# Weight sums of the up projection's quarters on GpSimd, and a third pair of tiles by quarters in the two middle passes

## The chip, the cores and the metric

The kernel runs on one core of a Trainium2 chip. The metric is device time in microseconds (us). TensorE is called PE here, VectorE DVE, ScalarE ACT, GpSimd POOL and SyncE SP, as in the profile.

## What is computed

A decoder trunk of two layers on 512 tokens of width 1024, in float32. Each layer runs four token mixers side by side on one projection of the normalised input, merges them with gates, and then an MLP with 4096 hidden columns. The change is in the MLP's first matrix:

```python
def squared_relu_mlp(h, w_up, w_down):
    return jnp.square(jax.nn.relu(h @ w_up)) @ w_down
...
        h = rms_norm(x, ln_mlp[l])
        x = x + squared_relu_mlp(h, w_up[l], w_down[l])
```

## The kernel before

**Precision.** A float32 weight chunk is loaded (`raw` or `cr`) and split in two: `whi` is its rounded part, written by ACT (a CAST), and `wlo` the rest, written by DVE as `raw - whi` (`split_w`, line 258). The activations are split too (`hh`/`hl` going in, `ah`/`al` between the matrices). Each product is three matmuls, hi by hi, lo by hi and hi by lo (`mm3`, line 268). There are three buffers each for `whi` and `wlo`, so a split waits until PE has finished with the chunk three before it.

**The MLP** (`mlp`, line 389) goes over the hidden columns in four passes (`PASSES`). A pass makes four pairs of 128-column tiles, t = 0 to 3 (the up part), and then multiplies them with their rows of `w_down` (the down part). The down part is always by quarters, the Strassen-Winograd way: seven products (forms) of half-size blocks in place of eight, with the names A11, S1, S2, S4, S3, A22, A12 in that order. Its blocks of weights are `chain`, `b22`, `sum2` and `raw`. Its four results per pass, c12, c22, c21, c11, are pairs of tiles `co` (three buffers in turn). In passes 1 and 2 they are added to a DRAM tensor by DMAs on POOL's queue (`keep`, line 556, `sum_dram<-co`), in pass 0 written by SP; pass 3 folds them into the output.

**The up part.** An ordinary pair is two tiles of 24 matmuls of 512 columns (lines 493 to 500). A pair whose number is in `SEVEN[p]` goes by quarters (`up_seven`, line 417). Its weights are four 128x512 blocks B11, B12, B22, B21, which SP loads into halves of four `cr` buffers; the other halves take weight sums:

```python
437  sums = {0: ((S1w, B11, B12),), 1: ((S2w, S1w, B22),), 2: ((S3w, B12, B22), (all4, S2w, B21)), 3: ()}
...
442                            for o_, a_, b_ in sums[i]:
443                                with HP():
444                                    V.tensor_add(o_, a_, b_)
445                            ws[i] = split_w(R[i], 512 if i == 3 else 1024, P)
```

So buffer R[0] holds B11 and S1w, R[1] S2w and B22, R[2] S3w and all4, R[3] B21 and B12. Each of the seven forms is 12 matmuls of 256 columns: A11 and S1 use R[0], S2 and S4 R[1], S3 and A22 R[2], A12 R[3]. Between forms, DVE and ACT move partial results out of PSUM: U = copy of A11's bank A, then at line 463 `V.tensor_sub(U2, C, U)`, in the profile `U<-up,U`, which reads bank C after S2 and before S3 adds into that bank; then the parts of F, relu and square. For every pair ACT and DVE then form the split activations: `ah`, `Fs`, `al` (lines 502 to 508).

**What sets the order.** Each engine works through its own queue in order. The order within a queue is made by a scheduler when the program is built; operations under `HP()` (high priority) are placed as early as it can. `cr` buffers (`CRB` = 6) are handed on by the scheduler too: a load into one waits until the split of what it held has ended.

Of the kernel before, what the change touches and what calls it, by code (L numbers as in the profile page):

```python
# [17 lines left out]
ALU = mybir.AluOpType  # L18
# [16 lines left out]
G1K = ((1, 1, 2, 2, 2), (2, 2, 2, 2))  # L35
KORD = ((0, 1, 2, 3, 4, 5, 6, 7), (4, 5, 6, 7, 0, 1, 2, 3))
PASSES = (8, 8, 8, 8)
SEVEN = ((2, 3), (2, 3), (2, 3), (2,))
CRB = 6
BIG = 1e30  # L40

# [12 lines left out]
def chunk_plan(l):  # L54
# [30 lines left out]
    for p, nt in enumerate(PASSES):  # L85

        half = nt // 2 * P
        for t in range(0, half, P):
            parts = 2 if t // P in SEVEN[p] else 1
            for i in range(parts):  # L90
# [80 lines left out]
def trunk(tc, x_in, wall, consts, lps, sgus, out):  # L171
    nc = tc.nc
    at = dict(mm=None, side=False, first=None)
    V, S, G, T_ = (Paced(tc, e, at) for e in (nc.vector, nc.scalar, nc.gpsimd, nc.tensor))
    HP = lambda off=URGENT: tc.high_priority(offset=off)
    plan = [ch for l in range(NL) for ch in chunk_plan(l)]
    with ExitStack() as es:
# [14 lines left out]
        def mmtile(name, tag="mm", bank=None):  # L192
            if bank is None:
                bank = turn[tag]
                turn[tag] = (bank + 1) % 4
            return psum.tile([P, 512], F32, name=name, tag=f"{tag}{bank}")
# [49 lines left out]
        def next_w(raw=None):  # L246
            kk, n = chunk_shape(plan[pos[0]])
            pos[0] += 1
            L = kk * n
            if raw is None:  # L250
                raw = wpool.tile([P, WCH], F32, name="raw", tag="raw", bufs=WB[0])
            src = wall[off[0]:off[0] + P * L].rearrange("(p l) -> p l", l=L)
            off[0] += P * L
            with HP():
                nc.sync.dma_start(raw[:, :L], src)
            return split_w(raw, L, n, V.tensor_copy if pos[0] == 1 else S.copy)

        def split_w(raw, L, n, copy=S.copy):
            hi = wpool.tile([P, WCH], F32R, name="whi", tag="whi", bufs=WB[1])
            lo = wpool.tile([P, WCH], F32R, name="wlo", tag="wlo", bufs=WB[1])  # L260
            with HP():
                copy(hi[:, :L], raw[:, :L])
                r = V.tensor_sub(lo[:, :L], raw[:, :L], hi[:, :L].bitcast(F32))
            at["first"] = r if pos[0] == 1 else None
            return (hi[:, :L].rearrange("p (k n) -> p k n", n=n),
                    lo[:, :L].rearrange("p (k n) -> p k n", n=n))

        def mm3(o, ah, al, bh, bl, start, stop, more=False):

            T_.matmul(o, ah, bh, start=start, stop=False, skip_group_check=more)  # L270
            T_.matmul(o, ah, bl, start=False, stop=False, skip_group_check=more)
            r = T_.matmul(o, al, bh, start=False, stop=stop, skip_group_check=more)
            if not at["side"]:
                at["mm"] = r
# [11 lines left out]
        def tick():  # L286
            at["side"] = True
            for g in list(side):
                if next(g, side) is side:
                    side.remove(g)  # L290
            at["side"] = False
# [97 lines left out]
        def mlp(l, hh, hl, r2, gain, fp, sh, sl):  # L389
# [9 lines left out]
            sums = sum_dram[l]  # L399
            with tc.tile_pool(name="ap", bufs=1) as ap:  # L400
# [6 lines left out]
                def cr():  # L407
                    return ap.tile([P, 1024], F32, name="cr", tag="cr", bufs=CRB)

                def moving(f, k):  # L410

                    if f >= S3:
                        return sh[k][:, f - S3], sl[k][:, f - S3]
                    k, r = k + 4 * (f in (A22, A12)), (row2, row1)[f in (A11, A12)]
                    return hh[k][:, r], hl[k][:, r]

                def up_seven(F):

                    base, sz = off[0], P * 512
                    off[0] += 4 * sz  # L420
                    pos[0] += 4

                    def ld(dst, i, j):
                        o = base + ((i - 1) * 2 + j - 1) * sz
                        with HP():
                            nc.sync.dma_start(dst, wall[o:o + sz].rearrange("(p l) -> p l", l=512))

                    R = [cr() for _ in range(4)]
                    R[1:] = R[2:] + R[1:2]
                    lo, up = slice(0, 512), slice(512, 1024)  # L430
                    B11, S1w, S2w, B22 = R[0][:, lo], R[0][:, up], R[1][:, lo], R[1][:, up]
                    S3w, all4, B21, B12 = R[2][:, lo], R[2][:, up], R[3][:, lo], R[3][:, up]
                    ld(B11, 1, 1)
                    ld(B12, 1, 2)
                    ld(B22, 2, 2)
                    ld(B21, 2, 1)
                    sums = {0: ((S1w, B11, B12),), 1: ((S2w, S1w, B22),), 2: ((S3w, B12, B22), (all4, S2w, B21)), 3: ()}
                    ws = [None] * 4

                    def form(f, o, i, n, first=True):  # L440
                        if ws[i] is None:
                            for o_, a_, b_ in sums[i]:
                                with HP():
                                    V.tensor_add(o_, a_, b_)
                            ws[i] = split_w(R[i], 512 if i == 3 else 1024, P)
                        w_h, w_l = ws[i]
                        for k in range(4):
                            bh, bl = moving(f, k)
                            mm3(o, w_h[:, 4 * n + k], w_l[:, 4 * n + k], bh, bl, first and k == 0, k == 3, not first)
                        tick()  # L450

                    A, B, C, E = (mmtile("up", "ms")[:, 0:256] for _ in range(4))
                    s1, s2 = (hpool.tile([P, 2, 256], F32, name="U", tag=n) for n in ("acc", "sq"))
                    U, U2, W, R5 = s1[:, 0], s1[:, 1], s2[:, 0], s2[:, 1]
                    form(A11, A, 0, 0)
                    with HP():
                        S.copy(U, A)
                    form(S1, B, 0, 1)
                    with HP():
                        S.copy(R5, B)  # L460
                    form(S2, C, 1, 0)
                    with HP():
                        V.tensor_sub(U2, C, U)
                    form(S4, B, 1, 1, False)
                    with HP():
                        V.tensor_add(F[:, A12], B, U2)
                    form(S3, C, 2, 0, False)
                    with HP():
                        V.tensor_sub(W, C, U)
                        V.tensor_add(F[:, A22], W, R5)  # L470
                        S.activation(F[:, 2:4], F[:, 2:4], AF.Relu)
                    form(A22, E, 2, 1)
                    with HP():
                        V.tensor_sub(F[:, A21], E, W)
                        S.activation(F[:, A21], F[:, A21], AF.Relu)
                    form(A12, A, 3, 0, False)
                    with HP():
                        S.activation(F[:, A11], A, AF.Relu)
                        S.activation(F, F, AF.Square)

                for p, nt in enumerate(PASSES):
                    nk = nt // 2
                    ah, al = [], []
                    for t in range(nk):
# [4 lines left out]
                        if t == 1:  # L489
                            early = at["mm"]  # L490
                        if t in SEVEN[p]:
                            up_seven(F)
                        for i in range(0 if t in SEVEN[p] else 2):
                            w_h, w_l = next_w()
# [1101 lines left out]
```

## Time and profile before

| | us |
|---|---|
| median of 3 runs | 1584.31 (1582.98 to 1584.33) |
| the profiled execution | 1584.03 |
| its span | 1582.3 |
| passes 0 to 2 of the first layer's MLP | 81.7, 80.9, 80.9 |
| POOL busy in the whole span | 144.9 |

Times inside the profile are us from the start of the span. A row of instructions has start, duration, engine, line, operation, out<-in, and in brackets the idle time ahead of it with what ended it. L143 is a helper that issues all instructions of the wrapped engines, so rows are told apart by tile names. A duration of PE is modelled and overlaps the next; the spacing of starts tells its pace. Of DVE and ACT the next instruction starts some 0.08 us before the last has ended.

### The profile page before, as it was taken

What the parts mean: (1) busy time and instruction counts of PE and PEld (TensorE: products, weight loads), DVE (VectorE), ACT (ScalarE), POOL (GpSimd) and SP (SyncE); (2) the same over time, 40 slices, a digit from 0 to 9 for tenths busy, and PEclk for the clock granted to TensorE, in tenths of its full rate; (3) what the DMA queues carried; (4) which work ended last, traced back from release to release, by engine and by line L of the source; (5) the groups of instructions that cost most, each with busy time, mean ns of one, the idle gap of its engine ahead of it and who ended that gap; (6) DMA issues with size and microseconds to landing.
All of it is one profiled execution on the core that took longest, in us unless ns stands there. A gap on an engine that the chain in (4) does not pass through costs nothing.

```text
span 1582.3 us, 21761 instructions
## 1 busy us (share of the span) xinstructions
PE 1573.6 (99%) x8091; PEld 1318.2 (83%) x8091; DVE 1226.1 (77%) x2103; ACT 753.9 (48%) x1160; POOL 144.9 (9%) x189
## 2 busy tenths in 40 slices
PE   9999999999999999999999999999999999999999
PEld 7888887888889898988888888887888888889887
DVE  6899997645588777785978999976555887868678
ACT  5553224423357464746545433254233574747462
POOL 1322000000001011111013120000000010111110
PEclk9999999999999999999999999999999999999999
DMA  7533322332347566769455233233223555676692
GB/s 193 146 91 102 101 97 88 104 116 97 104 153 202 166 172 139 198 135 270 131 131 140 81 113 105 84 101 134 86 97 108 172 160 180 167 166 180 145 281 81
DMA packets 77835, 218.22 MB, mean 138 GB/s; under 512 B 8832, under 2 KB 16192, under 8 KB 77728
## 3 DMA queue, kind: packets, MB, share of 16 engines
q1 hardware_dynamic: 60784, 175.54, 34.2%
q0 software_dynamic: 16080, 40.27, 13.0%
q8 instruction: 64, 1.05, 0.3%
q10 hardware_dynamic: 864, 1.01, 0.2%
q14 instruction: 43, 0.35, 0.1%
HBM read 192.10 MB, written 21.01 MB: 135 GB/s over the span
## 4 chain that ended last, share of the span: by engine, by line
PE 71%; DVE 16%; issue 5%; ACT 5%; DMA 2%; POOL 1%; SPq 0%; DVEq 0%; POOLq 0%; ACTq 0%
PE g L143 18%; PE up L143 15%; PE r L143 8%; PE tk L143 7%; PE q L143 6%; PE fm L143 5%; PE p L143 4%; PE wo L143 4%; DVE wlo L143 4%; DVE sco L143 2%; ACT whi L143 2%; DMA raw<-in_wall_dram 1%; DVE Fs L143 1%; DVE m L143 1%; ACT F L143 1%
## 5 line engine op out<-in xcount | busy, mean ns | idle before, releaser
L143 ACT CAST whi<-raw 128x1024 fp32r<-128x1024 f32 (+3 forms) x208 | 228.5, 1100 | 220.6 <-DMA raw<-in_wall_dram 81.7
L143 DVE TENSOR_TENSOR wlo<-raw,whi 128x1024 fp32r<-128x1024 f32 (+3 forms) x209 | 267.6, 1281 | 77.5 <-ACT whi L143 65.2
L143 PE MATMUL g<-hh,whi 128*128 128x512 f32 x512 | 200.6, 392 | 0.0
L143 PE MATMUL g<-hh,wlo 128*128 128x512 f32 x512 | 199.6, 390 | 0.0
L143 PE MATMUL g<-hl,whi 128*128 128x512 f32 x512 | 199.3, 389 | 0.0
L143 DVE TENSOR_TENSOR wlo<-cr,whi 128x1024 fp32r<-128x1024 f32 (+1 forms) x136 | 157.8, 1165 | 45.7 <-ACT whi L143 45.4
L143 ACT CAST whi<-cr 128x1024 fp32r<-128x1024 f32 (+1 forms) x136 | 136.9, 1008 | 105.4 <-PE up L143 40.4
L143 PE MATMUL up<-hh,whi 128*128 128x512 f32 (+1 forms) x456 | 160.4, 352 | 0.0
L143 PE MATMUL up<-hl,whi 128*128 128x512 f32 (+1 forms) x456 | 159.6, 350 | 0.0
L143 PE MATMUL up<-hh,wlo 128*128 128x512 f32 (+1 forms) x456 | 159.6, 350 | 0.0
L143 ACT ACTIVATE gs<-gs 128x512 f32<-128x512 f32 x64 | 40.6, 634 | 200.7 <-DVE gs L143 200.6
L143 PEld LDWEIGHTS g<-hh,wlo 128*128 128x128 f32 x512 | 96.1, 188 | 20.3
L143 PEld LDWEIGHTS g<-hh,whi 128*128 128x128 f32 x512 | 96.1, 188 | 19.8 <-issue 0.2
L143 PEld LDWEIGHTS g<-hl,whi 128*128 128x128 f32 x512 | 96.2, 188 | 19.3
L143 PE MATMUL tk<-whi,hh 128*128 128x512 f32 (+2 forms) x304 | 108.1, 359 | 0.0
L143 PE MATMUL tk<-wlo,hh 128*128 128x512 f32 (+2 forms) x304 | 107.1, 354 | 0.0
L143 PE MATMUL tk<-whi,hl 128*128 128x512 f32 (+2 forms) x304 | 106.3, 352 | 0.0
L143 DVE TENSOR_TENSOR gs<-g,rb 128x512 f32<-128x512 f32 x64 | 44.1, 688 | 78.8 <-PE g L143 78.7
L143 PE MATMUL q<-whi,ah 128*128 128x512 f32 (+1 forms) x260 | 100.7, 391 | 0.1
L143 PE MATMUL q<-whi,al 128*128 128x512 f32 (+1 forms) x260 | 99.8, 389 | 0.1
L143 PE MATMUL q<-wlo,ah 128*128 128x512 f32 (+1 forms) x260 | 99.6, 387 | 0.0
L143 PEld LDWEIGHTS up<-hh,whi 128*128 128x128 f32 x456 | 86.2, 189 | 12.6 <-ACT F L143 1.0
(308 smaller groups left out, 3556.1 us busy)
## 6 DMA issues: line engine op xcount, KB each, us to landing
raw<-in_wall_dram SPq DMA_DIRECT2D x135, 512.0 KB, 3.7
raw<-in_wall_dram SPq DMA_DIRECT2D x64, 640.0 KB, 3.8
cr<-in_wall_dram POOLq DMA_DIRECT2D x48, 512.0 KB, 8.3
cr<-in_wall_dram SPq DMA_DIRECT2D x32, 512.0 KB, 5.5
cr<-in_wall_dram SPq DMA_DIRECT2D x56, 256.0 KB, 2.9
sum_dram<-co POOLq DMA_DIRECT2D x32, 256.0 KB, 6.0
x<-in_x_dram SPq DMA_DIRECT2D x16, 256.0 KB, 5.1
xm_dram<-x SPq DMA_DIRECT2D x16, 256.0 KB, 2.0
```

Of the source, the lines that this page charges most:

```text
L143: r = f(*a, **k)
```

## The change

The four sums of a pair move from DVE to GpSimd and are issued together, after the loads and ahead of all forms, at high priority. And in passes 1 and 2 of each layer pair t = 1 goes by quarters too, so that a middle pass has one ordinary pair and three by quarters.

```diff
-SEVEN = ((2, 3), (2, 3), (2, 3), (2,))
+SEVEN = ((2, 3), (1, 2, 3), (1, 2, 3), (2,))
...
-                    sums = {0: ((S1w, B11, B12),), 1: ((S2w, S1w, B22),), 2: ((S3w, B12, B22), (all4, S2w, B21)), 3: ()}
+                    with HP():
+                        for o_, a_, b_ in (S1w, B11, B12), (S2w, S1w, B22), (S3w, B12, B22), (all4, S2w, B21):
+                            G.tensor_tensor(o_, a_, b_, ALU.add)
                     ws = [None] * 4
 
                     def form(f, o, i, n, first=True):
                         if ws[i] is None:
-                            for o_, a_, b_ in sums[i]:
-                                with HP():
-                                    V.tensor_add(o_, a_, b_)
                             ws[i] = split_w(R[i], 512 if i == 3 else 1024, P)
```

GpSimd's queue in the first layer, from the chain loads of pass 1 to those of pass 2, before (L538 adds a second block of `w_down` onto a loaded one, L540 loads one, L563 adds results to the sums in DRAM):

```order
L538 DMA cr<-in_wall_dram 128x1024
L540 DMA cr<-in_wall_dram 128x1024
L538 DMA cr<-in_wall_dram 128x1024
L540 DMA cr<-in_wall_dram 128x1024
L538 DMA cr<-in_wall_dram 128x1024 x2
L563 DMA sum_dram<-co 128x512 x8
L538 DMA cr<-in_wall_dram 128x1024
L540 DMA cr<-in_wall_dram 128x1024
```

The same place with the change, where the source's line numbers are one less:

```order
L143 TENSOR_TENSOR cr<-cr 128x512 x12
L537 DMA cr<-in_wall_dram 128x1024
L539 DMA cr<-in_wall_dram 128x1024
L537 DMA cr<-in_wall_dram 128x1024
L539 DMA cr<-in_wall_dram 128x1024
L537 DMA cr<-in_wall_dram 128x1024 x2
L143 TENSOR_TENSOR cr<-cr 128x512 x4
L562 DMA sum_dram<-co 128x512 x4
L143 TENSOR_TENSOR cr<-cr 128x512
L562 DMA sum_dram<-co 128x512 x4
L143 TENSOR_TENSOR cr<-cr 128x512 x7
L537 DMA cr<-in_wall_dram 128x1024
```

All twelve sums of pass 1 now stand ahead of its chain loads, and the four sums of pass 2's first pair stand ahead of the writes of pass 1's c12 and c22.

DVE's queue in pass 0, where the up part goes over from ordinary tiles to its first pair by quarters (`cr<-cr 128x512` are sums, `U<-up,U` is line 463), before:

```order
L143 TENSOR_TENSOR Fs<-F,Fs 128x256
L143 TENSOR_TENSOR cr<-cr 128x512 x2
L143 TENSOR_TENSOR al<-Fs,ah 128x1024
L143 TENSOR_TENSOR wlo<-cr,whi 128x1024
L143 TENSOR_TENSOR cr<-cr 128x512 x2
L143 TENSOR_TENSOR wlo<-cr,whi 128x1024
L143 TENSOR_TENSOR Fs<-F 128x512
L143 TENSOR_TENSOR Fs<-F,Fs 128x256
L143 TENSOR_TENSOR al<-F,ah 128x768
L143 TENSOR_TENSOR Fs<-F,Fs 128x256
L143 TENSOR_TENSOR wlo<-cr,whi 128x512
L143 TENSOR_TENSOR U<-up,U 128x256
```

The same place with the change:

```order
L143 TENSOR_TENSOR Fs<-F,Fs 128x256
L143 TENSOR_TENSOR al<-Fs,ah 128x1024
L143 TENSOR_TENSOR wlo<-cr,whi 128x1024 x2
L143 TENSOR_TENSOR Fs<-F 128x512
L143 TENSOR_TENSOR Fs<-F,Fs 128x256
L143 TENSOR_TENSOR al<-F,ah 128x768
L143 TENSOR_TENSOR Fs<-F,Fs 128x256
L143 TENSOR_TENSOR wlo<-cr,whi 128x512
L143 TENSOR_TENSOR U<-up,U 128x256
```

The sums are gone from DVE's queue and the rest keeps its order. In the second and third pair of a middle pass it is the same: two `wlo`, `Fs`, `Fs`, `al`, `Fs`, then `U`.

DVE's queue at the end of pass 1, from c12 (`co<-q`) over c22 (`co<-Z`) to the splits for the last A22 and A12 forms, before:

```order
L143 SCALAR_TENSOR_TENSOR co<-q_5388,t_61,U 128x512
L143 TENSOR_TENSOR wlo<-cr,whi 128x1024
L143 TENSOR_TENSOR cr<-cr 128x512 x3
L143 SCALAR_TENSOR_TENSOR Z<-r_5389,t_61,Z 128x512
L143 TENSOR_TENSOR wlo<-raw,whi 128x1024
L143 TENSOR_TENSOR co<-Z 128x512
L143 SCALAR_TENSOR_TENSOR Z<-r_5390,t_61,Z 128x512
L143 TENSOR_TENSOR wlo<-cr,whi 128x1024
L143 TENSOR_TENSOR co<-Z 128x512
L143 TENSOR_TENSOR wlo<-raw,whi 128x1024
```

With the change:

```order
L143 SCALAR_TENSOR_TENSOR co<-q_5451,t_61,U 128x512
L143 TENSOR_TENSOR wlo<-cr,whi 128x1024
L143 TENSOR_TENSOR wlo<-raw,whi 128x1024
L143 SCALAR_TENSOR_TENSOR Z<-r_5452,t_61,Z 128x512
L143 SCALAR_TENSOR_TENSOR Z<-r_5453,t_61,Z 128x512
L143 TENSOR_TENSOR co<-Z 128x512 x2
L143 TENSOR_TENSOR wlo<-cr,whi 128x1024
L143 TENSOR_TENSOR wlo<-raw,whi 128x1024 x2
```

The second tile of c22 now stands ahead of the `wlo<-cr` of the last A22 form, where it stood behind it.

## The prediction

> **What bounds the kernel now.** I read the page first, then the busy time of the four up/down passes of the first layer, then the instructions around one pair of tiles. Columns of the second block: stretch, its length, busy time and count of PE, PEld, DVE, ACT, POOL, then clock, DMA share, GB/s.
>
> ```profile
> span 1582.3 us, 21761 instructions
> PE 1573.6 (99%) x8091; PEld 1318.2 (83%) x8091; DVE 1226.1 (77%) x2103; ACT 753.9 (48%) x1160; POOL 144.9 (9%) x189
> ```
> ```profile
> 463.10:544.84 81.74, 81.53 (x449) 70.02 (x448) 70.76 (x95) 48.57 (x67) 4.68 (x6) 1.00 0.58 171
> 544.84:625.77 80.93, 80.71 (x433) 69.51 (x433) 62.21 (x78) 46.76 (x62) 7.93 (x10) 1.00 0.63 169
> 625.77:706.71 80.94, 80.72 (x434) 69.52 (x433) 63.25 (x79) 47.79 (x63) 13.13 (x16) 1.00 0.67 166
> ```
>
> The last two are the middle passes that get a third pair. What one matmul costs PE is read from starts, since the durations overlap (start, duration in us):
>
> ```profile
> 706.54 0.39 PE L143 MATMUL up<-hh,whi 128*128 128x512 f32 x1
> ...
> 728.30 0.28 PE L143 MATMUL up<-hh,whi 128*128 128x256 f32 x1
> 728.42 0.28 PE L143 MATMUL up<-hl,whi 128*128 128x256 f32 x1
> ```
>
> From the first up matmul of a pass to the first 256-wide one are 96 matmuls of 512 columns: 21.76/96 = 0.2267 us each. A 256-wide one follows after 0.12 us. A middle pass has 96 up matmuls of 512, 168 of 256 (two pairs of 84) and 168 down matmuls of 512: 264 x 0.2267 + 168 x 0.12 = 80.0 us of its 80.9. So PE sets the pace and only 0.9 us of a pass is waiting. VectorE (DVE) is not far off, though, and while a pair by quarters runs it has no room. This is the second pair of such a pass, on DVE and then PE:
>
> ```profile
> 573.60 1.22 DVE L143 TENSOR_TENSOR wlo<-cr,whi 128x1024 fp32r<-128x1024 f32 x1
> ...
> 578.27 1.23 DVE L143 TENSOR_TENSOR wlo<-cr,whi 128x1024 fp32r<-128x1024 f32 x1 [0.81 <-ACT whi L143]
> 579.41 0.68 DVE L143 TENSOR_TENSOR Fs<-F 128x512 f32<-128x512 f32 x1
> ...
> 580.48 0.95 DVE L143 TENSOR_TENSOR al<-F,ah 128x768 fp32r<-128x768 f32 x1
> 581.34 0.42 DVE L143 TENSOR_TENSOR Fs<-F,Fs 128x256 f32<-128x256 f32 x1
> 581.68 0.42 DVE L143 TENSOR_TENSOR U<-up,U 128x256 f32<-128x256 f32 x1
> ```
> ```profile
> 582.48 0.28 PE L143 MATMUL up<-sh,whi 128*128 128x256 f32 x1
> ```
>
> From 578.27 on DVE never waits. Its U (line 463) reads the PSUM bank that the form S3 then adds into, and S3 is the matmul at 582.48. U ends at 582.10: **0.38 us of slack**. Whatever delays DVE by more than that between 578 and 582 stops PE.
>
> **The change part by part.**
>
> *The third pair.* An ordinary pair is 48 matmuls of 512 columns, 48 x 0.2267 = 10.88 us; by quarters it is 84 of 256, 84 x 0.12 = 10.08. Saving 0.80 us, in two passes of two layers: **-3.2 us**, as PE sets the pace there. But two pairs by quarters in a row have a seam, since the next pair's first form needs the bank that ScalarE has yet to empty:
>
> ```profile
> 576.99 0.28 PE L143 MATMUL up<-sl,whi 128*128 128x256 f32 x1
> 577.11 0.28 PE L143 MATMUL up<-sh,wlo 128*128 128x256 f32 x1
> 577.36 0.38 PE L143 MATMUL up<-hh,whi 128*128 128x256 f32 x1
> 577.58 0.28 PE L143 MATMUL up<-hl,whi 128*128 128x256 f32 x1
> ```
>
> From 577.11 to 577.58 stand two matmuls in 0.47 us where 0.24 is usual: 0.23 us per seam. Three pairs have two seams instead of one: 4 x 0.23 = **+0.9 us**. The loads carry the same bytes (four of 256 KB for two of 512 KB) and come early; ScalarE, busy 47 of 81 us, gets four more operations per pair and hides them.
>
> *The sums on GpSimd.* Four 128x512 adds per pair leave DVE, where one takes about 0.6 us of its queue (two in the 1.29 us row below). GpSimd has this shape as a multiply, beside DVE operations whose usual time is the last row's:
>
> ```profile
> 136.41 1.30 POOL L143 TENSOR_TENSOR wt<-wt,cst 128x512 f32<-128x512 f32 x1 [3.90 <-issue]
> ```
> ```profile
> 136.48 2.03 DVE L143 SCALAR_TENSOR_TENSOR X<-X,c_gc,bigT 128x128 f32<-128x128 f32 x3
> ```
> ```profile
> 923.07 1.47 POOL L143 TENSOR_TENSOR wt<-wt,cst 128x512 f32<-128x512 f32 x1 [3.73 <-DMA wt<-in_sgus_dram]
> ```
> ```profile
> 922.77 1.92 DVE L143 SCALAR_TENSOR_TENSOR X<-X,c_gc,bigT 128x128 f32<-128x128 f32 x3
> 924.99 0.33 DVE L143 SCALAR_TENSOR_TENSOR X<-X,c_gc,bigT 128x128 f32<-128x128 f32 x1
> ```
>
> Three X operations of 0.33 us should take about 1.0 us; both times they took 1.9 to 2.0 when a GpSimd multiply began among them, and 0.9 to 1.0 us went. So a GpSimd operation on two SBUF tensors holds up a DVE operation on two SBUF tensors: I take **1.0 us lost per add that meets a busy DVE**, against 0.6 when DVE did the add itself. Bounds: 0, where DVE would have waited anyway, and 1.30, the whole add. The Trainium skill ("SBUF — State Buffer", section "SBUF: two separate sides") says why: VectorE and GpSimd share a port pair, locked for a whole instruction against a VectorE operation with two SBUF inputs. By that rule the loss would be the whole 1.30 us, and the term of the middle passes below 12 us instead of 8.4; the two rows show about 1.0, and the measurement stands.
>
> Where do the adds fall? Those of the first pair of a pass fall in the pass before, where the buffers come free; there DVE has some 2 us of slack ahead of PE, and I count nothing. Those of the second pair fall beside the ordinary tiles: nothing. Those of the new third pair can't come early. The second add needs the load into the buffer that the split at 573.60 (ended 574.82) gives free, and a load takes 2.9 us:
>
> ```profile
> cr<-in_wall_dram SPq DMA_DIRECT2D x56, 256.0 KB, 2.9
> ```
>
> So it starts at 577.7 at the earliest, and with the third and fourth 1.30 us each behind it the three reach to 581.6, exactly the stretch in which DVE runs wlo, Fs, Fs, al and Fs, all on two SBUF tensors, in front of U. The split that could go at 578.27 gets through some 1.0 us after 577.7, so loses 0.45; the other two cost 1.0 each: 2.45 us, less 0.38 of slack, is **2.1 us of PE waiting** per middle pass: **+8.4 us** for four (0 to 0.75 + 1.3 + 1.3 - 0.38 = 3.0 each, so 0 to 12). In the third pair no add is left, and DVE is level with PE again. ScalarE's cast of each buffer now waits for GpSimd's add in place of DVE's, with the relu and square of the tiles queued behind it; the third pair's third buffer, the one that needs the fourth add, is split a whole pair, 10 us, after the second pair's (at 578.27), so even an add that ends at 583 is in time.
>
> *The first pass of a layer* (two pairs, as before). Here the last two adds of the second pair sit in the DVE queue right in front of the first U:
>
> ```profile
> 485.47 1.29 DVE L143 TENSOR_TENSOR cr<-cr 128x512 f32<-128x512 f32 x2
> 486.68 1.22 DVE L143 TENSOR_TENSOR wlo<-cr,whi 128x1024 fp32r<-128x1024 f32 x1
> ...
> 490.69 0.42 DVE L143 TENSOR_TENSOR U<-up,U 128x256 f32<-128x256 f32 x1
> ```
> ```profile
> 491.20 0.35 PE L143 MATMUL up<-sh,whi 128*128 128x256 f32 x1
> ```
>
> They go (1.2 us), and as GpSimd adds that wait for the same split they meet DVE's queue (2.0 us): 0.8 later, less 0.1 of slack: 0.7, twice: **+1.4 us** (0 to 2.6).
>
> *GpSimd's queue.* At the end of a middle pass four adds now stand ahead of the writes of c12 to the sums in DRAM. DVE's second c22 tile reuses c12's buffer, and DVE's order has it ahead of the split for the second A22 form:
>
> ```profile
> 609.24 0.86 POOL L563 DMA_DIRECT2D sum_dram<-co  x1 [20.39 <-DVE co L143]
> ```
> ```profile
> 608.86 1.21 DVE L143 TENSOR_TENSOR wlo<-cr,whi 128x1024 fp32r<-128x1024 f32 x1
> ...
> 617.78 0.68 DVE L143 TENSOR_TENSOR co<-Z 128x512 f32<-128x512 f32 x1
> ```
> ```profile
> sum_dram<-co POOLq DMA_DIRECT2D x32, 256.0 KB, 6.0
> ```
> ```profile
> 620.33 2.72 PE r L143 x12
> ```
>
> The third add waits for the split that ends at 610.07, so the fourth ends at about 612.7, and the first write leaves 3.5 us later than 609.24. Landed 6.0 us on, at 618.7, it lets c22 go (0.6) and then the split (1.2): 620.5, against PE's need at 620.33. So nothing if the write lands 0.2 us sooner than the median, and 1.1 if the splits that the adds meet there cost them 0.9 us; I take 0 per middle pass, as 0.2 is the nearer.
>
> **The sum**: -3.2 + 0.9 + 8.4 + 1.4 = +7.5 us. The profiled execution took 1584.03 us (its span of 1582.3 and 1.7 around it); the median of three is 1584.31, 0.3 above. So 1584.03 + 7.5 + 0.3 = **1591.8 us**.
>
> **The rivals.** About 0.2%, 3.2 us, is what a measurement of this kernel can tell from no change.
>
> *A, the adds are hidden and PE's saving counts.* If GpSimd gets its turns where DVE waits for ScalarE (such as the 0.81 us ahead of 578.27), only -3.2 + 0.9 = -2.3 us remains: 1582.0. For it: DVE is idle 18 us of a middle pass. Against: none of these gaps lies between 578.27 and U. It decides for A if the three adds cost DVE less than the 0.38 us of slack. Chance 0.20.
>
> *B, GpSimd's queue decides as well.* If the writes of c12 land 1.1 us too late in each of four middle passes, 4.4 us come on top: 1596.2. For it: DVE's order puts c22 in front of the split. Against: two of the four adds there fall beside DVE operations on PSUM. Chance 0.12.
>
> *C, DVE's relief reaches further.* At the start of S2 in the down part PE waits for DVE's split:
>
> ```profile
> 598.12 0.39 PE L143 MATMUL r<-whi,ah 128*128 128x512 f32 x1
> 598.73 0.50 PE L143 MATMUL r<-wlo,ah 128*128 128x512 f32 x1 [0.22 <-DVE wlo L143]
> ```
>
> These starts lie 0.61 us apart where 0.23 is usual, so 0.38 us is lost, and the down part of six passes has this form; if the adds' leaving closes all six and A holds, 1582.0 - 2.3 = 1579.7. Against: no add stood in DVE's queue just ahead of it. Chance 0.08.
>
> That the change does not do what it says is out: the built order has the adds on GpSimd and the third pair's 256-wide matmuls.
>
> "Perfetto Trace Analysis" of the Trainium skill, section "Optimizing Scalar/DVE Operations", says that moving work between these two engines might not help since they share an SBUF read port; it speaks for the forecast over A.
>
> **How the numbers follow.** My forecast has 0.60, by itself 1586 to 1597 (middle passes 1 to 3 us each). The range 1581.5 to 1600 takes in A and B, and leaves out C and the case of all upper bounds at once. Faster by over 0.2%: C and an edge of A, 0.11; within: the rest of A, 0.17; slower: 0.72.
>
> **What would show it.** In the changed profile: middle passes of about 82.5 us instead of 80.9; GpSimd adds of about 1.3 us; in the second pair of three, Fs or al of over 1.5 us beside them, U about 2 us late, and PE idle ahead of a 256-wide up matmul with DVE's U as releaser. If the middle passes are 80.3 us and those DVE operations keep their times, A is right. If PE's wait lies ahead of the last A22 form of the down part, B is. I am wrong in principle if an add beside a DVE operation costs it nothing.

## The result and the profile after

The changed kernel takes 1606.41 us (median of 4 runs, 1606.17 to 1612.91) where the kernel before takes 1584.32: ratio 1.0149, 95% interval 1.0133 to 1.0164. That is 22.1 us slower; the forecast was 7.5 us slower.

The page of the changed kernel, its span, its busy times and the new group on POOL:

```profile
span 1604.5 us, 22215 instructions
PE 1577.0 (98%) x8235; PEld 1327.3 (83%) x8235; DVE 1247.3 (78%) x2075; ACT 760.2 (47%) x1176; POOL 258.8 (16%) x261
...
L143 POOL TENSOR_TENSOR cr<-cr 128x512 f32<-128x512 f32 x72 | 113.9, 1601 | 671.6 <-DMA cr<-in_wall_dram 622.6
```

An add takes 1.6 us on average, and DVE, which lost 72 adds, is busier than before (1247 against 1226 us). Where PE waits stands in the view of waits of the changed kernel (total, times, longest):

```profile
PE up L143 <- DVE U L143: 15.6, 8, 2.8
...
PE up L143 <- ACT U L143: 1.5, 2, 0.9
```

So it is U that PE waits for, as forecast, but for 15.6 us, eight times. The stretches of the first layer's passes 0, 1 and 2 (columns as in the prediction):

```profile
463.34:547.72 84.38, 82.10 (x450) 70.12 (x448) 70.79 (x83) 48.23 (x68) 25.09 (x19) 1.00 0.56 169
547.72:630.50 82.78, 80.50 (x469) 70.72 (x468) 65.31 (x77) 48.88 (x66) 24.58 (x21) 1.00 0.60 160
630.50:717.54 87.04, 82.27 (x470) 72.27 (x468) 69.99 (x78) 48.61 (x66) 30.18 (x27) 0.98 0.60 151
```

| pass, both layers | before | after | more | forecast |
|---|---|---|---|---|
| 0 | 81.8, 81.7 | 84.4, 84.7 | +2.6, +3.0 | +0.7 each |
| 1 | 80.9, 80.9 | 82.8, 82.8 | +1.9 each | +1.5 each |
| 2 | 80.9, 80.9 | 87.0, 86.8 | +6.1, +5.8 | +1.5 each |
| 3 and all the rest | | | +1.0 together | 0 |

Pass 1 went nearly as forecast. This is its second pair, the same place as in the prediction: DVE, then the adds on POOL, then PE's form S3:

```profile
570.73 1.43 DVE L143 TENSOR_TENSOR wlo<-cr,whi 128x1024 fp32r<-128x1024 f32 x1 [0.81 <-ACT whi L143]
572.08 1.79 DVE L143 TENSOR_TENSOR Fs<-F 128x512 f32<-128x512 f32 x1
573.90 1.40 DVE L143 TENSOR_TENSOR Fs<-F,Fs 128x256 f32<-128x256 f32 x1
575.23 0.94 DVE L143 TENSOR_TENSOR al<-F,ah 128x768 fp32r<-128x768 f32 x1
...
576.43 0.41 DVE L143 TENSOR_TENSOR U<-up,U 128x256 f32<-128x256 f32 x1
```
```profile
569.72 5.30 POOL L143 TENSOR_TENSOR cr<-cr 128x512 f32<-128x512 f32 x3 [1.55 <-DMA cr<-in_wall_dram]
```
```profile
576.89 0.39 PE L143 MATMUL up<-sh,whi 128*128 128x256 f32 x1 [1.79 <-DVE U L143]
```

The three adds took 5.30 us (three that meet no DVE work, at 555.56, took 3.79), and beside them wlo took 0.21 us more than before (1.43 for 1.22), the first Fs 1.11 more (1.79 for 0.68) and the second 0.98 more (1.40 for 0.42): 2.30 us, less the slack of 0.38, makes 1.92. The start of S3 is 1.95 us late.

Pass 2 has one more wait that the forecast did not have, in its first pair by quarters. The load into the second pair's third buffer on SP (the expectations below call it the fifth buffer's load), the adds that wait for it, DVE beside them, PE, and the clock behind it:

```profile
636.31 0.33 SPq L426 DMA_DIRECT2D cr<-in_wall_dram  x1
```
```profile
644.14 4.71 POOL L143 TENSOR_TENSOR cr<-cr 128x512 f32<-128x512 f32 x3 [6.56 <-DMA cr<-in_wall_dram]
```
```profile
644.37 1.40 DVE L143 TENSOR_TENSOR Fs<-F,Fs 128x256 f32<-128x256 f32 x1
645.69 2.04 DVE L143 TENSOR_TENSOR al<-F,ah 128x768 fp32r<-128x768 f32 x1
647.66 1.48 DVE L143 TENSOR_TENSOR Fs<-F,Fs 128x256 f32<-128x256 f32 x1
...
649.66 0.41 DVE L143 TENSOR_TENSOR U<-up,U 128x256 f32<-128x256 f32 x1
```
```profile
647.02 0.28 PE L143 MATMUL up<-sh,wlo 128*128 128x256 f32 x1
650.12 0.39 PE L143 MATMUL up<-sh,whi 128*128 128x256 f32 x1 [2.83 <-DVE U L143]
```
```profile
650.98:654.18 3.20, 3.20 (x17) 3.20 (x16) 3.17 (x5) 0.19 (x1) 1.50 (x1) 0.50 0.53 171
```

The same load and its adds in pass 1:

```profile
551.57 0.33 SPq L426 DMA_DIRECT2D cr<-in_wall_dram  x1
```
```profile
555.56 3.79 POOL L143 TENSOR_TENSOR cr<-cr 128x512 f32<-128x512 f32 x3 [8.58 <-DMA cr<-in_wall_dram]
```

In pass 2 the load is issued at 636.31 and the add that waits for it starts at 644.14, 7.8 us later. In pass 1 it is issued at 551.57 and its add starts at 555.56, 4.0 us later, well ahead of the first pair's Fs and al. The issue comes later too: 5.8 us behind the first up matmul of its pass (630.50), where pass 1 has 3.9 (547.72). Of the 5.8 us by which the adds are later in their pass, 2.0 stand ahead of the issue and 3.8 behind it. So in pass 2 the three adds fall among the first pair's Fs and al and cost DVE 0.98 + 1.09 + 1.06 = 3.1 us, and S3 is 2.99 us late. Behind this wait PE works with half its clock (0.50) for 3.2 us: 256-wide matmuls start 0.213 us apart in place of 0.12, which costs another 16 x 0.093 = 1.5 us. Both come in pass 2 of either layer: together 9.0 us.

In pass 0 five adds stand beside the ordinary tile's split activations, on DVE and then ACT and PE:

```profile
477.28 1.77 DVE L143 TENSOR_TENSOR Fs<-F 128x512 f32<-128x512 f32 x1
479.08 1.40 DVE L143 TENSOR_TENSOR Fs<-F,Fs 128x256 f32<-128x256 f32 x1
480.40 2.04 DVE L143 TENSOR_TENSOR al<-F,ah 128x768 fp32r<-128x768 f32 x1
482.36 1.51 DVE L143 TENSOR_TENSOR Fs<-F,Fs 128x256 f32<-128x256 f32 x1
```
```profile
483.90 1.05 ACT L143 CAST ah<-Fs 128x1024 fp32r<-128x1024 f32 x1 [5.79 <-DVE Fs L143]
```
```profile
490.99 0.39 PE L143 MATMUL up<-sh,whi 128*128 128x256 f32 x1 [0.62 <-ACT U L143]
...
494.15 0.39 PE L143 MATMUL up<-sh,whi 128*128 128x256 f32 x1 [1.47 <-DVE U L143]
```

DVE loses 1.09 + 0.98 + 1.09 + 1.09 = 4.2 us here. ACT waits 5.79 us for the last Fs with the casts and relus of the next tiles queued behind it, and PE pays twice, for ACT's copy U and for DVE's U.

### The profile page after: what moved, and what is told of

Same layout as the page of the kernel before. It is cut to its first block, busy times and chain, and to the rows that moved or that the text cites. A ratio compares the mean times of both kernels' runs of the same rounds, so it can differ in the third digit from the quotient of the medians.

```text
span 1604.5 us, 22215 instructions
## 1 busy us (share of the span) xinstructions
PE 1577.0 (98%) x8235; PEld 1327.3 (83%) x8235; DVE 1247.3 (78%) x2075; ACT 760.2 (47%) x1176; POOL 258.8 (16%) x261
## 3 DMA queue, kind: packets, MB, share of 16 engines
q8 instruction: 65, 1.06, 0.3%
## 4 chain that ended last, share of the span: by engine, by line
PE 70%; DVE 16%; issue 6%; ACT 6%; DMA 1%; POOL 1%; SPq 0%; ACTq 0%; DVEq 0%; POOLq 0%
PE g L143 18%; PE up L143 9%; PE tk L143 8%; PE r L143 8%; PE q L143 7%; PE fm L143 6%; PE wo L143 5%; PE p L143 5%; DVE wlo L143 4%; DVE Fs L143 3%; ACT whi L143 3%; DVE sco L143 2%; ACT F L143 1%; DVE al L143 1%; DVE m L143 1%
## 5 line engine op out<-in xcount | busy, mean ns | idle before, releaser
L143 ACT CAST whi<-raw 128x1024 fp32r<-128x1024 f32 (+3 forms) x200 | 220.0, 1102 | 204.4 <-DMA raw<-in_wall_dram 86.8
L143 DVE TENSOR_TENSOR wlo<-raw,whi 128x1024 fp32r<-128x1024 f32 (+3 forms) x201 | 261.7, 1303 | 67.4 <-ACT whi L143 64.3
L143 DVE TENSOR_TENSOR wlo<-cr,whi 128x1024 fp32r<-128x1024 f32 (+1 forms) x152 | 183.9, 1214 | 69.6 <-ACT whi L143 69.3
L143 POOL TENSOR_TENSOR cr<-cr 128x512 f32<-128x512 f32 x72 | 113.9, 1601 | 671.6 <-DMA cr<-in_wall_dram 622.6
L143 ACT CAST whi<-cr 128x1024 fp32r<-128x1024 f32 (+1 forms) x152 | 151.9, 1001 | 112.4 <-PE r L143 37.8
L143 PE MATMUL up<-hh,whi 128*128 128x512 f32 (+1 forms) x440 | 150.7, 342 | 0.6 <-ACT F L143 0.5
L143 PE MATMUL up<-hl,whi 128*128 128x512 f32 (+1 forms) x440 | 149.4, 340 | 0.0
L143 PE MATMUL up<-hh,wlo 128*128 128x512 f32 (+1 forms) x440 | 149.4, 339 | 0.0
L143 PE MATMUL up<-sh,whi 128*128 128x256 f32 x288 | 82.9, 288 | 17.1 <-DVE U L143 15.6
```

The lines of the kernel that those rows point to most:

```text
L143: r = f(*a, **k)
```

## The experiments

All ratios are against the kernel before on the same chip (medians there 1585.7 to 1586.2).

**What holds DVE up: the adds' reads.** Each add is replaced by a memset of the same half buffer.

```diff
-                            G.tensor_tensor(o_, a_, b_, ALU.add)
+                            G.memset(o_, 0.0)
```

> The changed kernel with each GpSimd add replaced by a memset of the same 128x512 half buffer, so GpSimd reads nothing of SBUF there and does not wait for the loads (the sums are left out: the output is not the reference's). Theory L: VectorE's Fs, al and wlo keep their usual 0.68, 0.42, 0.95 and 1.22 us, no wait ahead of S3 is left, and only the third pair's saving remains: about 1582 us, middle passes about 80.4 us. Rival Q (GpSimd's queue, its place ahead of the writes and the chain loads, makes the loss): the middle passes stay at 82.8 and 86.9 us, about 1600 us or more.

Measured: ratio 0.9980 (0.9971 to 0.9989), 3.2 us faster than before. Passes 1 and 2, and DVE in the first pair of pass 2 with a memset beside the first row (640.71, 0.53 us):

```profile
546.98:627.45 80.47, 80.22 (x470) 70.66 (x468) 61.74 (x77) 47.74 (x65) 15.78 (x24) 1.00 0.63 169
627.45:707.91 80.46, 80.21 (x469) 70.66 (x468) 61.77 (x77) 49.80 (x67) 17.02 (x25) 1.00 0.66 164
```
```profile
640.58 0.69 DVE L143 TENSOR_TENSOR Fs<-F 128x512 f32<-128x512 f32 x1
641.31 0.42 DVE L143 TENSOR_TENSOR Fs<-F,Fs 128x256 f32<-128x256 f32 x1
```

No wait of PE for U is left. In the whole trace 14 operations of DVE on two SBUF tensors (6 Fs and 8 wlo) have a memset beside them and keep their usual times. A third pair is worth 0.46 us per middle pass (forecast 0.57). A memset neither reads nor waits for a load, so this run alone doesn't tell the two apart; the next one does.

```diff
-                            G.tensor_tensor(o_, a_, b_, ALU.add)
+                            G.tensor_copy(o_, b_)
```

> The changed kernel with each GpSimd add replaced by a copy of its second input, one SBUF tensor read in place of two (the sums are left out: the output is not the reference's). Theory L1 (any GpSimd operation that reads SBUF holds up VectorE's operations on two SBUF tensors for its whole length): Fs, al and wlo beside a copy are longer by about the copy's own length, and the waits ahead of S3 shrink only as far as a copy is shorter than an add of 1.28 us; if it takes 0.9 us, about 1590 to 1597 us. Theory L2 (only two reads hold it up): those operations keep their usual times, middle passes about 80.5 us, about 1582 us.

Measured: 1.0004 (0.9995 to 1.0013), 1586.68 us, which lies between the times of both theories. A copy takes 0.61 us undisturbed. The three late copies of pass 2, and DVE beside them:

```profile
638.04 2.38 POOL L143 COPY cr<-cr 128x512 f32<-128x512 f32 x3 [6.98 <-DMA cr<-in_wall_dram]
```
```profile
638.11 1.08 DVE L143 TENSOR_TENSOR Fs<-F 128x512 f32<-128x512 f32 x1
639.23 0.71 DVE L143 TENSOR_TENSOR Fs<-F,Fs 128x256 f32<-128x256 f32 x1
639.87 1.36 DVE L143 TENSOR_TENSOR al<-F,ah 128x768 fp32r<-128x768 f32 x1
```

L1's mechanism holds, with its price lower than written: one read is enough, and each copy costs DVE 0.3 to 0.4 us (1.08 for 0.69, 0.71 for 0.42, 1.36 for 0.95). An add costs 1.0 to 1.1 of its 1.28. So in these traces a GpSimd operation that reads SBUF holds a DVE operation on two SBUF tensors for its own length less 0.2 to 0.3 us.

**The two halves of the change alone.** First the sums on GpSimd with the pairs as before.

```diff
-SEVEN = ((2, 3), (1, 2, 3), (1, 2, 3), (2,))
+SEVEN = ((2, 3), (2, 3), (2, 3), (2,))
```

> The sums on GpSimd, pairs by quarters as before (two in the middle passes). Theory L (a GpSimd add and a VectorE operation on two SBUF tensors hold each other up, so each add that falls among Fs, al and wlo costs VectorE about 1.0 us ahead of U): pass 0 of each layer +2.8 us as in the changed kernel, and the middle passes lose as well, since the second pair's late adds still fall into the first pair's stretch: about +2.0 each, so 1584.3 + 5.6 + 1.0 (outside the MLP passes) + 8.0 = about 1599 us. Rival T (the third pair makes the loss in the middle passes; with two pairs the adds hide beside the ordinary tiles): only pass 0 and the rest, 1584.3 + 6.6 = about 1591 us.

Measured: 1.0053 (1.0036 to 1.0070), 8.4 us: nearer to T. Pass 0 took 84.4 and 85.0 us, the middle passes 81.0, 82.0, 83.5 and 82.0, so with two pairs most adds fall where DVE has slack. The 83.5 holds a wait of the forecast's rival B, at the start of the last A22 form (DVE, then PE):

```profile
1415.20 0.69 DVE L143 TENSOR_TENSOR co<-Z 128x512 f32<-128x512 f32 x1 [3.98 <-DMA sum_dram<-co]
```
```profile
1417.09 0.50 PE L143 MATMUL r<-wlo,ah 128*128 128x512 f32 x1 [2.22 <-DVE wlo L143]
```

Then the third pair with the sums on DVE (the kernel before with the other `SEVEN`).

> The third pair by quarters, the sums on VectorE as before. Theory D (VectorE has no room for sums while one pair by quarters follows another: its operations of such a pair add up to about 10 us of the pair's 10.08, and the four sums add 2.4): PE saves 2.3 us in all, each middle pass loses up to 2.0 us ahead of U, so up to 1584.3 - 2.3 + 8.0 = 1590 us, with pass 0 unchanged at 81.7 us. Rival R (VectorE catches up in the down part, and the third pair's saving counts): 1584.3 - 2.3 = 1582.0 us.

Measured: 1.0055 (1.0038 to 1.0071), 8.7 us, more than D's 5.7, and not in D's place. The loss stands in pass 2 (85.3 and 85.0 us) and hardly in pass 1 (81.4 and 81.3), in the first pair. DVE, then PE:

```profile
638.43 0.69 DVE L143 TENSOR_TENSOR cr<-cr 128x512 f32<-128x512 f32 x1 [7.83 <-DMA cr<-in_wall_dram]
```
```profile
645.98 0.58 PE L143 MATMUL up<-sh,whi 128*128 128x256 f32 x1 [2.61 <-DVE U L143]
```

The same late load: here the sum that needs it stands in DVE's queue, 7.8 us behind the issue at 630.63, with everything up to U behind it. So the wait in pass 2's first pair belongs to the third pair and needs no sums on GpSimd.

**Why the load is late in pass 2.** The first theory was that the adds hold up GpSimd's writes, and these the load. The adds of passes 2 and 3 were put behind the writes (`kept` lists the eight writes of the pass before):

```diff
-                            G.tensor_tensor(o_, a_, b_, ALU.add)
+                            r = G.tensor_tensor(o_, a_, b_, ALU.add)
+                            if p > 1:
+                                behind = kept[3 if t == SEVEN[p][0] else 7]
+                                tc.add_manual_dep(ins_of(r), ins_of(behind).name, V._dep, reason="pace")
...
-                                nc.gpsimd.dma_start(dst, tiles[b], accum_op=ALU.add)
+                                kept.append(nc.gpsimd.dma_start(dst, tiles[b], accum_op=ALU.add))
```

> The changed kernel with the sums of passes 2 and 3 put behind the writes in GpSimd's queue: those of the pass's first pair by quarters behind the four writes of c12 and c22, the others behind all eight. Theory W (in pass 2 the writes held up behind the adds crowd the loads, the fifth buffer's load takes 7.7 us in place of 3.8, and the second pair's adds so fall among Fs and al of the first): pass 2 comes down from 87.0 to pass 1's 82.8 us, in all 1606.4 - 8.4 = about 1598 us. Rival B2 (the adds fall late in pass 2 for another reason, the buffers or ScalarE's order): pass 2 stays at 87 us, in all 1605 to 1607 us.

Measured: 1.0172 (1.0147 to 1.0196). Theory W falls: pass 2 takes 87.4 and 86.2 us, and the adds wait as long for the load (issued at 638.01):

```profile
645.83 4.72 POOL L143 TENSOR_TENSOR cr<-cr 128x512 f32<-128x512 f32 x3 [3.91 <-DMA cr<-in_wall_dram]
```

Next, the loads of 512 KB that stand ahead of it on SP's queue, moved behind it:

```diff
-                        load(raw[:, :1024], 1, 1, k)
+                        load(raw[:, :1024], 1, 1, k, behind=early)
```

> The changed kernel with the two loads of 512 KB for the down part's A11 form issued behind the load of the up part's fifth buffer, not ahead of it at the pass's start. Theory C (the fifth buffer's load of 256 KB takes 7.7 us in pass 2, against 3.8 in pass 1, because it shares the DMA engines with such a load of 512 KB; so the second pair's adds come late and fall among Fs and al of the first): it lands in about 4 us, the 3.0 us wait and the half clock behind it (1.5 us) go, pass 2 takes 83 us, in all 1606.4 - 8 = about 1598 us. Rival A (the four accumulating writes of c21 and c11 alone make it slow): it still takes 7 us or more and pass 2 stays at 86 to 87 us, in all about 1606 us.

Measured: 1.0150 (1.0129 to 1.0170), pass 2 at 85.6 and 86.6 us. The load now takes 5.9 us from issue (636.85) to the add (642.75), so half of the 3.8 us that it took longer than in pass 1 is gone. But it is issued as late in its pass as before, 5.8 us behind the first up matmul (631.10), and the wait ahead of S3 is still 2.7: these loads have a share, and taking it away is not enough. Last, pass 1's writes without accumulation, on SP's queue in place of GpSimd's:

```diff
-                            if p == 0:
+                            if p <= 1:
                                 nc.sync.dma_start(dst, tiles[b])
```

> The changed kernel with pass 1's four results written by SP over what lies in DRAM, as pass 0's are, in place of GpSimd's accumulating writes (the adding of pass 1 to pass 0 is left out: the output is not the reference's). Theory A (the accumulating writes of pass 1's results, still under way at the start of pass 2, make the fifth buffer's load take 7.7 us): it lands in about 4 us as in pass 1, the second pair's adds come before Fs and al of the first, and pass 2 takes pass 1's 82.8 us: 1606.4 - 8 = about 1598 us. Rival P (something else in pass 2, the buffers that come free in another order or the writes as such): pass 2 stays at 86 to 87 us, about 1606 us.

Measured: 1.0092 (1.0074 to 1.0111), 1601.37 us. That is 9 us less than the changed kernel by the two ratios, and 6 by the medians, each over its own kernel before. Pass 2 of both layers, then the load and its adds in the first:

```profile
632.24:715.16 82.92, 80.60 (x470) 70.67 (x468) 65.80 (x77) 47.90 (x66) 24.80 (x21) 1.00 0.57 154
...
1428.05:1512.13 84.08, 81.73 (x469) 72.14 (x468) 66.26 (x77) 48.16 (x66) 25.19 (x22) 0.98 0.56 151
```
```profile
635.11 0.33 SPq L426 DMA_DIRECT2D cr<-in_wall_dram  x1
```
```profile
640.71 3.79 POOL L143 TENSOR_TENSOR cr<-cr 128x512 f32<-128x512 f32 x3 [10.25 <-DMA cr<-in_wall_dram]
```

The first pair's wait is gone in both (84.08 holds a half-clock stretch behind its second pair's wait, and so do pass 1's 84.2 and 84.4 us here). The load still takes 5.6 us, not 4, but it is issued 2.9 us behind the first up matmul (632.24) and not 5.8, so its adds start 5.2 us earlier in the pass than in the changed kernel: 2.9 from the issue, 2.2 from the load's own time. The issue moves for the same reason: it stands behind the splits of an earlier load of 512 KB (`raw`), which is 6.7 us under way in the changed kernel (issued at 625.59) and 4.5 here (626.62). So theory A holds in this sense: GpSimd's accumulating writes make the loads beside them late, this one and the one before it. Whether the adding does it or the queue is not shown, since the plain writes also went to another queue. The DMA queues of the changed kernel from 636.3 to 644, and in pass 1 from 551.5 to 555.5 (packets, MB, share of 16 engines):

```profile
q0 software_dynamic: 364, 0.65, 53.1%
q1 hardware_dynamic: 288, 0.79, 33.4%
```
```profile
q1 hardware_dynamic: 531, 1.19, 85.2%
```

The accumulating queue (q0) fills 53% of the engines to move 0.65 MB, the loads (q1) 33% to move 0.79: about twice the engines' time for each MB.

**Pass 0.** Its sums alone went back to DVE.

```diff
-                            G.tensor_tensor(o_, a_, b_, ALU.add)
+                            (V if p == 0 else G).tensor_tensor(o_, a_, b_, ALU.add)
```

> The changed kernel with the sums of pass 0 alone back on VectorE, in one place ahead of the forms. Theory L (the eight adds beside VectorE's work of the ordinary tiles cost pass 0 its 2.6 and 3.0 us): pass 0 back to about 81.8 us, 1606.4 - 5.6 = about 1601 us. Rival O (the place of the sums, all together ahead of the forms, costs pass 0 and not the engine that makes them): pass 0 stays at 83 us or more, 1604 to 1607 us.

Measured: 1.0128 (1.0112 to 1.0144), 1606.33 us. Pass 0 of both layers, and pass 2 of the first:

```profile
464.52:546.96 82.44, 81.79 (x449) 70.04 (x448) 69.81 (x91) 48.49 (x68) 12.08 (x11) 1.00 0.59 173
...
631.64:720.19 88.55, 83.77 (x470) 73.73 (x468) 69.92 (x77) 48.60 (x66) 30.20 (x27) 0.96 0.61 149
1262.49:1344.21 81.72, 81.51 (x449) 69.99 (x448) 70.37 (x92) 49.74 (x69) 12.65 (x11) 1.00 0.58 176
```

Theory L is right for pass 0: 82.4 and 81.7 us, 1.9 and 3.0 less. The whole kernel did not get as much faster, because PE ran at half clock five times in this profile where the changed kernel did twice (3 x 1.5 = 4.5 us). The profile is no exception: all four runs had mean clocks of 0.995 to 0.996, three of the changed kernel's four 0.997 to 0.998.

**A better place for the third pair.** Pair 0 in place of pair 1, so that an ordinary pair stands behind it; once with all sums on DVE and once with pair 0's sums on GpSimd.

```diff
-SEVEN = ((2, 3), (2, 3), (2, 3), (2,))
+SEVEN = ((2, 3), (0, 2, 3), (0, 2, 3), (2,))
...
-                                    V.tensor_add(o_, a_, b_)
+                                    (G if t == 0 else V).tensor_tensor(o_, a_, b_, ALU.add)
```

> The sums on VectorE as before; the third pair by quarters is t = 0 in place of t = 1, so the ordinary pair stands between the first and the second. Theory D (VectorE has no room only where one pair by quarters follows another): the third pair's 0.8 us per middle pass is kept, no further seam, 1584.3 - 3.2 = about 1581 us. Rival S (at the start of a pass VectorE is still behind with the down part's last splits and results, so U of pair 0 comes late): 1 to 2 us in each middle pass eat the saving, 1585 to 1589 us.

Measured: 1.0029 (1.0018 to 1.0040). Neither D nor S in full: pass 1 took 81.1 and 80.2 us, pass 2 85.8 and 82.1. In the 85.8 DVE again sits behind a sum that waits for a load:

```profile
639.00 0.69 DVE L143 TENSOR_TENSOR cr<-cr 128x512 f32<-128x512 f32 x1 [4.21 <-DMA cr<-in_wall_dram]
```

> As the kernel with pair 0 by quarters, with pair 0's four sums on GpSimd, where they fall into the down part of the pass before, and all other sums on VectorE. Theory L (an add on GpSimd costs only where VectorE has no slack ahead of PE; in the down part it has): as with all sums on VectorE or up to 1 us faster, 1580 to 1581 us. Rival B (the adds hold up the writes of c12 ahead of c22 and the split for the last A22 form, which in one pass of the kernel with only the sums moved cost 2.4 us): up to 4 us slower than with all sums on VectorE.

Measured: 1.0061 (1.0049 to 1.0074), 5 us slower than with all sums on DVE, more than rival B had. The wait stands at the start of pass 2, where PE needs the bank of a down result:

```profile
1418.44 0.36 PE L143 MATMUL up<-hh,whi 128*128 128x256 f32 x1 [2.83 <-DVE co L143]
```

That the adds held up the write that this `co` waits for is argued from GpSimd's order, not shown by a run of its own. With pair 0 in pass 1 only, away from the accumulating writes:

```diff
-SEVEN = ((2, 3), (2, 3), (2, 3), (2,))
+SEVEN = ((2, 3), (0, 2, 3), (2, 3), (2,))
```

> The kernel before with a third pair by quarters, t = 0, in pass 1 only, sums on VectorE. In the kernel with it in both middle passes, pass 1 of the second layer took 80.17 us where 80.93 is usual, pass 2 82.1 to 85.8, since loads come late there. Theory D and A together: pass 1 saves 0.8 us in each layer, nothing else moves: 1584.3 - 1.6 = about 1582.7 us, the fastest of the versions. Rival S (pass 1's gain is taken back by its own late loads, as in the first layer of that kernel, where it took 81.06): 1584 to 1585 us.

Measured: 0.9998 (0.9989 to 1.0007), no difference. Pass 1 took 80.15 us in the second layer and 80.93 in the first. There it looks like rival S: DVE's sums waited 0.5 and 2.3 us for loads (ahead of 547.80 and 554.77), against 0.4 and 1.2 in the second layer, and PE lost about 0.3 and 0.4 us behind them. That is read from the trace, not shown by a run of its own. No version that computes the whole beat the kernel before.

## Why the prediction was wrong

**Right: the sign, the mechanism and its place.** GpSimd's adds hold DVE up ahead of U, and PE waits for U in the second of three pairs. The price of an add (1.0 us) was measured at 1.0 to 1.1, the wait in pass 1 at 1.95 us where 2.1 was forecast, the third pair's net saving at 0.46 where 0.57 was. Rival A is out: beside a busy DVE an add is not hidden. C is out as well, since the wait at S2 stayed (0.38 us in the middle passes).

The Trainium skill ("SBUF — State Buffer", section "SBUF: two separate sides") has the loser wait for the whole instruction, and only against a GpSimd operation that reads SBUF. The runs agree on the second point (memset against copy); on the first they show 0.2 to 0.3 us less than the whole.

**Wrong, the step "Those of the second pair fall beside the ordinary tiles: nothing", and under it that the loads "come early".** The rows that it shows of a middle pass are all from pass 1, where both hold. In pass 2 these adds wait for a load that is issued 2.0 us later in the pass and is 7.8 us under way, fall among Fs and al of the first pair, and cost 3.0 us of waiting and, in the changed kernel's profile, 1.5 of half clock: 9.0 us for two layers, the larger part of the 14.6 that were missing. The forecast took the load's 2.9 us from a median over 56 loads; the one that mattered lies at the start of a pass, under pass 1's accumulating writes. The same load spoils the third pair even with all sums on DVE: the forecast's two terms for it, -3.2 and +0.9, came out at +8.7 us when it was measured alone.

**Wrong, the size in pass 0.** It counted two adds that meet DVE's queue: +0.7 us. But seven of the eight stand beside it, five of them in the ordinary tile's Fs and al, which had been counted as free. Through ACT's cast `ah<-Fs` that delay reaches the next pair: +2.6 and +3.0 us, 4.2 more than forecast.

**GpSimd's queue.** In the changed kernel rival B's wait did not come (0, as taken), but by luck: in pass 1 the first write was issued at 618.63, 6.4 us ahead of PE's last A22 form (625.06) where the forecast had 7.6, and let DVE go on at 622.60, after 4.0 us where the forecast took the median of 6.0. In the kernel with the sums alone the wait came once in four middle passes, 2.4 us, when the write issued at 1408.17 let DVE go on only at 1415.20, after 7.0. So it is a matter of a microsecond or two in a landing, as the small margin of 0.2 us had said.

The sum as measured, in the terms of the forecast: pass 0 +5.6, pass 1 +3.7, pass 2 +11.9, the rest +1.0, together +22.2, the difference of the two spans.

## What to carry to other kernels

Before work goes to GpSimd, mark every stretch where VectorE works on two SBUF tensors: there an add of 1.28 us cost VectorE about 1.05, against the 0.6 that it took on VectorE itself. Take the time at which a moved operation runs from each stage, not from the first of its kind: the same load took 4 us in one pass and 8 in the next, and was issued 2 us later in it. A gain of 0.8 us per pass is worth nothing if it brings an in-order queue to wait for a load that lands in a crowd.

## What the runs showed of the hardware that was not expected

- **A short wait can halve PE's clock.** Over the changed kernel and the experiments there are 42 waits of over 1.5 us between two 256-wide up matmuls, counted from start to start. None of the 13 under 2.0 us was followed by a half-clock stretch, 12 of the 24 from 2.0 to 2.96 us were (in one of them it began during the wait), and all 5 from 3.1 us on. The stretch costs about 1.5 us.
- **Where such a wait falls decides.** In every profile with several half-clock stretches these start whole multiples of 3.413 us apart (650.88 and 1449.60 in the changed kernel lie 234 of them apart) and last 3.41 us. Cut each profile into slices of that length, at those starts, and count as idle what a matmul starts later than the pace allows. In all 13 slices with more than 2.0 us idle (the end of the program aside) the next slice ran at half clock; after none with less than 1.88 did it; of the 10 between, it did after 6. So a wait of 2.01 us that lay within one slice was followed by a stretch (at 665.41, in the kernel with pass 0's sums on DVE), and one of 2.96 us that lay across two was not (1450.43, in the kernel with the writes first). The Trainium skill ("TensorE: Matmul & The Clock Gate", section "Part 1: The HAM clock gate") puts the drop after at least one idle window of about 3.4 us that runs freely. The fixed slices agree with a free-running window of that length; that some 1.9 to 2.0 us of idling in it are enough does not agree with a window that must be idle throughout.
- The same program's time goes with the number of such stretches: the four runs with plain writes took 1603.2, 1602.6, 1598.8 and 1600.1 us at mean clocks of 0.997, 0.998, 1.000 and 0.998.
- The hold works both ways: the adds themselves grew from 1.28 us to 1.6 on average. DVE's operations with a PSUM input keep their times beside an add (in the changed kernel 12 of `co<-q,t,U` with 0.74 us, 4 of `U<-up,U` with 0.42).
